# Token-row sums for three entrance norms, roots spread by a product of ones, and a square-root table for the last root

## The chip, the cores and the metric

One core of a Trainium2 chip runs the whole kernel. The metric is the device time of one execution in microseconds, the median of three timed runs. The engines are TensorE (PE; PEld are its weight loads), VectorE (DVE), ScalarE (ACT), GpSimd (POOL) and SyncE (SP), which issues nearly all DMA transfers.

## The reference

The input x has 2048 tokens of 1024 float32 values. One decoder block is computed:

```python
hn = rmsnorm(h, norm1_g)                       # h = x; mean of squares over the 1024 values of a token
proj = einsum('bsd,de->bse', hn, w_in)         # u_pool | q | k | v, 512 each
y_pool = pool_mixer(u_pool, pool_w, pool_scale)
o = stick_breaking_attention(q, k, v)          # 8 heads of 64
mixed = concatenate([rmsnorm(y_pool, pool_out_g), rmsnorm(y_attn, attn_out_g)])
h = h + einsum('bse,ed->bsd', mixed, w_out)
act = square(relu(einsum('bsd,df->bsf', rmsnorm(h, norm2_g), w_up)))
h = h + einsum('bsf,fd->bsd', act, w_down)
return rmsnorm(h, final_g)
# rmsnorm(x, g) = x * rsqrt(mean(x * x) + 1e-6) * g
```

## The kernel before

Tokens are cut into NT = 4 chunks of T = 512, and each chunk into TB = 4 blocks of P = 128. Activations are kept with the channels on the partitions and 512 tokens along the row, so a chunk of x is KD = 8 tiles of 128x512. Every matmul operand is split into a high and a low fp32r part (`split`, L145 to L148: a copy on ScalarE, a subtraction on VectorE), and a product is three matmuls (L179 to L181): one dense step, 24 matmuls of 512 columns, makes 128 output channels of one chunk. Only the needed near part of the attention is computed, unless a check at the end (L1636) asks for the rest; that branch does not run here.

Three stages follow each other: the front (input projection, pooling, near attention and their norms, up to about 500 us), the output projection (`tail`, to about 670 us), and the two feed-forward products (`up`, `down`), whose last steps (`last_steps`) end with the final norm of the last chunk and its output.

A norm over channels works across partitions. In the front, `norm1_rms(j)` squares the eight tiles of a chunk on ScalarE and adds them up on VectorE (`add_square`, L187 to L191). `mean_squares` (L207) multiplies the sum by a column of 1/n with four matmuls of one column, so that each token's mean stands on a partition. `inv_root` (L215 to L226) takes the root by three Newton steps on columns of 128x4, on GpSimd except for the first chunk and the last half. `spread` (L233) brings the four columns back along the rows for all partitions: eight matmuls of 128 columns, with a high and a low part, into one bank, which a ScalarE copy (L258) makes into the factor r. The pieces of h are then x times gain times r (`normed`, L278), split.

The names that the change touches: `norm1_rms` (chunks 1, 2 and 3; chunk 0 has `norm1_first`), `inv_root`, `inv_rms`, `to_all`, `later_rms`, `norm_parts` (the norms of the pooling output for all chunks and of the attention output; for attention chunks 2 and 3 it is called with `make`), `front`, and `last_turn` and `last_steps` in `down`. The accumulators of dense steps are two banks (`psd`), the spreads of the front use `pst` or `psz`, and the pool `ntp` of three 128x512 buffers holds squares and normed tiles alike.

What sets the order: the Tile framework plans every engine's order by priority (program order, raised in `tc.high_priority`) in a simulated timeline, and each engine then runs its list in that order, waiting on semaphores. `tc.issue_after(ins)` places what is written under it behind `ins`, but only on the engine of `ins`. The list `later` holds small steps of the norms; `catch_up` writes one to three of them behind each dense step, behind the last weight split and an earlier evacuation (`done[0]`). `load_x` puts the loads of xT behind the last weight load on SP; nothing else orders loads there but priority, buffers and data. Weights come through two `raw` buffers (SP) and five split granules `hl`, each good for 12 matmuls.

## Time and profile before

| | |
|---|---|
| timed runs, median (lowest to highest) | 1884.99 us (1883.61 to 1886.21) |
| profiled execution, its own time; its span | 1889.78 us; 1888.0 us |
| mean granted clock of TensorE | 0.997 |
| PE busy; PEld | 1863.1 us (99%); 1551.5 us (82%) |
| DVE; ACT; POOL busy | 1471.4 us (78%); 1025.8 us (54%); 226.4 us (12%) |
| DMA moved | 535.91 MB, mean 284 GB/s |
| chain that ended last, by engine | PE 81%, DMA 7%, DVE 7%, ACT 2%, issue 2% |

The page counts a matmul as busy to its modelled end, so neighbouring matmuls overlap, and a PE that is 99% busy can still have short holes; those are listed as waits. What one group of matmuls costs is read from the starts around it. Durations in a group are of single instructions; on ACT and DVE the next one can start before the last has ended.

### The profile page before, as it was taken

What the parts mean: (1) busy time and instruction counts of PE and PEld (TensorE: products, weight loads), DVE (VectorE), ACT (ScalarE), POOL (GpSimd) and SP (SyncE); (2) the same over time, 40 slices, a digit from 0 to 9 for tenths busy, and PEclk for the clock granted to TensorE, in tenths of its full rate; (3) what the DMA queues carried; (4) which work ended last, traced back from release to release, by engine and by line L of the source; (5) the groups of instructions that cost most, each with busy time, mean ns of one, the idle gap of its engine ahead of it and who ended that gap; (6) DMA issues with size and microseconds to landing.
All of it is one profiled execution on the core that took longest, in us unless ns stands there. A gap on an engine that the chain in (4) does not pass through costs nothing.

```text
span 1888.0 us, 26651 instructions
## 1 busy us (share of the span) xinstructions
PE 1863.1 (99%) x8883; PEld 1551.5 (82%) x8883; DVE 1471.4 (78%) x2135; ACT 1025.8 (54%) x1616; POOL 226.4 (12%) x463
## 2 busy tenths in 40 slices
PE   9999999999999999999999999999999999999997
PEld 7888888888888788888888888887888888888886
DVE  6887889678866877878799988886565677989774
ACT  6565666455644454555557555554333665656543
POOL 0232234112311040000000000000010010020120
PEclk9999999999999999999999999999999999999999
DMA  7686796899796858989798988889999898899852
GB/s 227 217 269 187 238 291 204 257 333 302 272 365 227 308 199 292 336 286 321 271 340 304 319 295 286 286 303 335 359 318 316 303 319 307 332 299 346 284 207 92
DMA packets 222164, 535.91 MB, mean 284 GB/s; under 512 B 26048, under 2 KB 32192, under 8 KB 218176
## 3 DMA queue, kind: packets, MB, share of 16 engines
q1 hardware_dynamic: 217264, 525.46, 80.4%
q0 software_dynamic: 4608, 8.39, 2.5%
q8 instruction: 72, 1.18, 0.3%
q14 instruction: 76, 0.62, 0.1%
q10 hardware_dynamic: 144, 0.26, 0.0%
HBM read 349.46 MB, written 184.55 MB: 283 GB/s over the span
## 4 chain that ended last, share of the span: by engine, by line
PE 81%; DMA 7%; DVE 7%; ACT 2%; issue 2%; POOL 1%; SPq 1%; DVEq 0%; ACTq 0%; POOLq 0%
PE pY L1148 17%; PE pb L1321 14%; PE pb L1498 12%; PE pZ L1148 8%; PE pd L179 6%; PE pd L181 6%; PE pd L180 6%; PE pX L1148 4%; PE po L702 1%; DMA ar<-sd 1%; PE pta L690 1%; DMA raw<-in_w_in_dram 1%; DVE hl L148 1%; DMA ar<-sdi 1%; DMA sr<-su 1%
## 5 line engine op out<-in xcount | busy, mean ns | idle before, releaser
L1148 PE MATMUL pY<-sa,hw 128*128 128x512 f32 x1536 | 366.1, 389 | 2.2 <-ACT u L1071 2.1
L1148 PEld LDWEIGHTS pY<-sa,hw 128*128 128x128 f32 x1536 | 287.9, 188 | 63.8 <-ACT u L1071 3.4
L1321 PE MATMUL pb<-ad,wd 128*128 128x512 f32 x1344 | 305.2, 389 | 0.3 <-DVE ad L148 0.3
L179 PE MATMUL pd<-h,hl 128*128 128x512 f32 x752 | 296.9, 395 | 4.4 <-DVE qk L148 2.4
L180 PE MATMUL pd<-h,hl 128*128 128x512 f32 x752 | 296.3, 394 | 0.0
L181 PE MATMUL pd<-h,hl 128*128 128x512 f32 x752 | 295.9, 394 | 0.0
L1321 PEld LDWEIGHTS pb<-ad,wd 128*128 128x128 f32 x1344 | 252.1, 188 | 53.1 <-DVE ad L148 0.7
L1498 PE MATMUL pb<-ad,wd 128*128 128x512 f32 x1104 | 253.9, 390 | 1.6 <-DVE ad L148 0.9
L1498 PEld LDWEIGHTS pb<-ad,wd 128*128 128x128 f32 x1104 | 206.6, 188 | 45.3 <-DVE ad L148 1.7
L148 DVE TENSOR_TENSOR ad<-ar,ad 128x1024 fp32r<-128x1024 f32 x160 | 194.0, 1221 | 38.8 <-ACT ad L147 38.4
L147 ACT ACTIVATE ad<-ar 128x1024 fp32r<-128x1024 f32 x160 | 168.9, 1057 | 93.9 <-PE pb L1498 38.2
L1148 PE MATMUL pZ<-sa,hw 128*128 128x512 f32 x768 | 185.9, 389 | 0.0
L1148 PEld LDWEIGHTS pZ<-sa,hw 128*128 128x128 f32 x768 | 144.0, 188 | 30.2 <-ACT sa L147 0.4
L147 ACT ACTIVATE hl<-raw 128x512 fp32r<-128x512 f32 x168 | 104.2, 629 | 117.6 <-PE pd L181 79.4
L179 PEld LDWEIGHTS pd<-h,hl 128*128 128x128 f32 x752 | 141.7, 188 | 32.0 <-DVE qk L148 2.8
L181 PEld LDWEIGHTS pd<-h,hl 128*128 128x128 f32 x752 | 141.6, 188 | 28.3
L180 PEld LDWEIGHTS pd<-h,hl 128*128 128x128 f32 x752 | 141.8, 189 | 26.1
L148 DVE TENSOR_TENSOR hl<-raw,hl 128x512 fp32r<-128x512 f32 x168 | 114.8, 689 | 50.3 <-ACT hl L147 49.0
L148 DVE TENSOR_TENSOR hw<-rt,hw 128x512 fp32r<-128x512 f32 x128 | 86.8, 686 | 33.1 <-ACT hw L147 33.1
L147 ACT ACTIVATE wd<-wq 128x1024 fp32r<-128x1024 f32 x56 | 59.5, 1063 | 76.1 <-PE pb L1321 65.7
L1065 ACT ACTIVATE a<-a 128x512 f32<-128x512 f32 x96 | 60.0, 629 | 74.1 <-DVE a L1107 35.9
L148 DVE TENSOR_TENSOR wd<-wq,wd 128x1024 fp32r<-128x1024 f32 x56 | 68.4, 1222 | 32.4 <-ACT wd L147 32.4
(224 smaller groups left out, 2712.0 us busy)
## 6 DMA issues: line engine op xcount, KB each, us to landing
ar<-sd SPq DMA_DIRECT2D x96, 512.0 KB, 5.8
ar<-sdi SPq DMA_DIRECT2D x64, 512.0 KB, 5.9
rb<-in_w_up_dram SPq DMA_DIRECT2D x30, 1024.0 KB, 6.8
sd<-a SPq DMA_DIRECT2D x104, 256.0 KB, 5.0
raw<-in_w_in_dram SPq DMA_DIRECT2D x50, 512.0 KB, 4.8
sdi<-hr SPq DMA_DIRECT2D x96, 256.0 KB, 5.2
wr<-in_w_down_dram SPq DMA_DIRECT2D x48, 512.0 KB, 5.5
sd<-s SPq DMA_DIRECT2D x88, 256.0 KB, 4.7
```

The lines of the kernel that those rows point to most:

```text
L147: nc.scalar.activation(hi, src, AF.Copy)
L148: return nc.vector.tensor_tensor(lo, src, hi.bitcast(F32), ALU.subtract)
L179: nc.tensor.matmul(ps, hl[:, 0, c], hi, start=(k == 0), stop=False)
L180: nc.tensor.matmul(ps, hl[:, 0, c], lo, start=False, stop=False)
L181: last_mm[0] = nc.tensor.matmul(ps, hl[:, 1, c], hi, start=False, stop=(k == n - 1))
L690: nc.tensor.transpose(pt[:, x * P:(x + 1) * P], sg[:, x * P:(x + 1) * P], ident)
L702: nc.tensor.matmul(po[0:m, p * 256 + to:p * 256 + to + hi - lo], vw[:, 2 * p + v, 0:m], at[:, x, lo:hi], start=(p == 0 and n == 0), skip_g ...
L1065: nc.scalar.activation(t, src, AF.Relu)
L1148: nc.tensor.matmul(t, w[:, wx, c], a[:, ax, c % 2], start=first and c == 0 and x == 0, stop=last and c == G - 1 and x == 2, skip_group_che ...
L1321: nc.tensor.matmul(b, t[:, wx, 2 * (kk % 2) + c, i * P:(i + 1) * P], a[:, ax, c], start=p in ("P1", "P5", "P2") and kk == 0 and c == 0 and ...
L1498: nc.tensor.matmul(ps[q, n], block(t, wx, c, n), left_[q][:, ax, c], start=(n_ in ("P1", "P3") and kk == 0 and c == 0 and x == 0), stop=(n ...
```

## The change

There are three edits.

First, `norm1_rms` for chunks 1 to 3. x is given a second time, as token rows (`x_rows`, blocks of 128 tokens by 1024 channels). Four loads of 512 KB per chunk go through one buffer (`xr`), and ScalarE squares each in place with a running sum over the row, which gives one column of sums. The root then starts from those four columns with the scale 1/n in its first step, on GpSimd. The eight squares, seven adds and the matmuls of `mean_squares` are left out for these norms. In `front` the note that writes this norm for chunk 1 moves one dense step ahead.

Second, `spread_rows`, for six norms (the pooling output of four chunks, the attention output of chunks 0 and 1). The root's columns are written into a zeroed 128x128 tile; one matmul against the identity turns them into rows, four ScalarE copies masked by a selector make a 128x512 tile that holds only the row of each block, and one matmul with a stationary matrix of ones adds high and low parts and spreads them. All other spreads stay as they were, reading the columns out of the zeroed tile.

Third, `root_by_table`, in `last_steps`: the root of the last norm's two halves takes a square root on ScalarE, a reciprocal and one Newton step on VectorE in place of three Newton steps. A square root of one column is put in front of `last_turn`.

Constants for this (`sel`, `oner`, `eps`, `sums1`, the two zeroed tiles) are made at the start.

```diff
@@ -51,14 +51,18 @@
...
-    wp = hpb = hpa = pa = bigp = x0p = ntp = tmp = att = psd = psx = psz = pst = pso = olp = accp = acc2p = acc3p = None
+    wp = hpb = hpa = pa = bigp = x0p = ntp = tmp = att = psd = psx = psz = pst = pso = olp = accp = acc2p = acc3p = wide = None
 
     def open_pools(scope):
-        nonlocal hpb, wp, tmp, ntp, psd, psx, psz, pst, pso
+        nonlocal hpb, wp, wide, tmp, ntp, psd, psx, psz, pst, pso
         fpool = lambda name, bufs, **kw: scope.enter_context(tc.tile_pool(name=name, bufs=bufs, **kw))
         hpb = fpool("hpb", KD, side="right")
         ntp = fpool("ntp", 3, side="right")
         tmp = fpool("tmp", 2, side="right")
+        wide = [tmp.tile([P, P], F32R, name=f"wide{i}", bufs=1) for i in range(2)]
+        tmp.tile([P, P // 2], F32, name="gap2", bufs=1)
+        for t in wide:
+            nc.gpsimd.memset(t.bitcast(F32), 0.0)
         wp = fpool("wp", 2, side="right")
         psz = fpool("psz", 2, space=PS)
         pso = fpool("pso", 1, space=PS)
@@ -96,7 +100,11 @@
     make_identity(nc, ident)
     identr = const.tile([P, P], F32R, name="identr")
     nc.vector.tensor_copy(identr, ident)
-    const.tile([P, P // 2], F32, name="gap")
+    const.tile([P, P // 2 - 40], F32, name="gap")
+    sel = const.tile([P, TB], F32, name="sel")
+    nc.vector.tensor_tensor(sel, ident[:, 0:TB], ident[:, TB:2 * TB], ALU.add)
+    oner = const.tile([P, TB], F32R, name="oner")
+    nc.vector.tensor_scalar(oner, sel, 0.0, 1.0, op0=ALU.mult, op1=ALU.add)
     later_keys = const.tile([P, 2, 2, P], mybir.dt.int8, name="later_keys")
     nc.gpsimd.memset(later_keys, 0.0)
     for i in range(2):
@@ -120,6 +128,9 @@
     rlast = const.tile([P, 2, T], F32, name="rlast")
     sslast = const.tile([P, T], F32, name="sslast")
     yrlast = const.tile([P, 2, 2, TB], F32R, name="yrlast")
+    sums1 = const.tile([P, NT, TB], F32, name="sums1")
+    eps = const.tile([P, 8], F32, name="eps")
+    nc.vector.memset(eps, EPS)
     carry = const.tile([P, len(WINDOWS), PAD], F32, name="carry")
     nc.vector.memset(carry, 0.0)
     window_sum = const.tile([P, len(WINDOWS)], F32, name="window_sum")
@@ -208,11 +219,11 @@
                                                start=(i == 0), stop=(i == len(parts) - 1))
         return pm[:, 0:TB]
 
-    def inv_root(pm, eng):
+    def inv_root(pm, eng, scale=None):
 
         v, w = vp.tile([P, 3 * TB], F32, tag="v", name="v"), pm.shape[-1]
         m, y, t = v[:, 0:w], v[:, TB:TB + w], v[:, 2 * TB:2 * TB + w]
-        nc.vector.tensor_scalar(m, pm, 1.0, EPS, op0=ALU.mult, op1=ALU.add)
+        (eng if scale else nc.vector).tensor_scalar(m, pm, scale or 1.0, EPS, op0=ALU.mult, op1=ALU.add)
         eng.tensor_scalar(y.bitcast(I32), m.bitcast(I32), -0.5, float(0x5F3759DF), op0=ALU.mult, op1=ALU.add)
         for _ in range(3):
             if eng is nc.vector:
@@ -226,6 +237,18 @@
                 eng.tensor_tensor(y, y, t, ALU.mult)
         return y
 
+    def root_by_table(pm):
+
+        v, w = vp.tile([P, 3 * TB], F32, tag="v", name="v"), pm.shape[-1]
+        m, y, t = v[:, 0:w], v[:, TB:TB + w], v[:, 2 * TB:2 * TB + w]
+        nc.scalar.activation(t, pm, AF.Sqrt, bias=eps[:, 0:1])
+        nc.vector.tensor_scalar(m, pm, 1.0, EPS, op0=ALU.mult, op1=ALU.add)
+        nc.vector.reciprocal(y, t)
+        nc.vector.scalar_tensor_tensor(t, y, -0.5, y, op0=ALU.mult, op1=ALU.mult)
+        nc.vector.tensor_tensor(t, t, m, ALU.mult)
+        nc.vector.scalar_tensor_tensor(y, t, 1.5, y, op0=ALU.add, op1=ALU.mult)
+        return y
+
     def spread(pr, yr):
 
         for b in range(TB):
@@ -234,37 +257,55 @@
                                       start=(b == 0 and x == 0), stop=(b == TB - 1 and x == 1), skip_group_check=True)
         return mm
 
+    def spread_rows(pr, yr, r):
+
+        nc.tensor.matmul(pr[:, 0:P], yr, identr, start=True, stop=True)
+        z = ntp.tile([P, T], F32R, tag="nt", name="roots")
+        for b in range(TB):
+            nc.scalar.activation(z[:, b * P:(b + 1) * P], pr[:, 0:P], AF.Copy, scale=sel[:, b:b + 1])
+        mm = nc.tensor.matmul(pr, oner[:, 0:1].to_broadcast([P, P]), z, start=True, stop=True)
+        nc.scalar.activation(r, pr, AF.Copy)
+        return mm
+
     def inv_rms(ss, n, r=None, eng=None, early=False):
 
         eng = eng or nc.gpsimd
         with tc.high_priority():
-            y = inv_root(mean_squares([ss], n, psz if early else None, "pz" if early else "px"), eng)
-            yr = tmp.tile([P, 2, TB], F32R, tag="yr", name="yr")
+            rows = ss.shape[-1] == TB
+            y = inv_root(ss, eng, 1.0 / n) if rows else inv_root(
+                mean_squares([ss], n, psz if early else None, "pz" if early else "px"), eng)
+            wide.append(wide.pop(0))
+            yr = wide[0][:, 0:2 * TB].rearrange("p (x b) -> p x b", x=2)
             eng.tensor_copy(yr[:, 0], y)
             eng.tensor_tensor(yr[:, 1], y, yr[:, 0].bitcast(F32), ALU.subtract)
             if eng is nc.vector:
                 return to_all(yr, r, psx, "px")
-            gates.append((state["tick"] + 10, marks["pm"]))
-            return yr
-
-    def to_all(yr, r, where, tag):
+            if not rows:
+                gates.append((state["tick"] + 10, marks["pm"]))
+            return wide[0]
+
+    def to_all(yr, r, where, tag, rows=False):
         with tc.high_priority():
             pr = where.tile([P, T], F32, tag=tag, name="pr")
-            marks["pr"] = spread(pr, yr)
-            if tag != "px":
-                gates.append((state["tick"] + 12, marks["pr"]))
             if r is None:
                 r = tmp.tile([P, T], F32, tag="r", name="r", bufs=2)
-            nc.scalar.activation(r, pr, AF.Copy)
+            if not rows:
+                marks["pr"] = spread(pr, yr[:, 0:2 * TB].rearrange("p (x b) -> p x b", x=2) if tag != "px" else yr)
+                if tag != "px":
+                    gates.append((state["tick"] + 12, marks["pr"]))
+                nc.scalar.activation(r, pr, AF.Copy)
+            else:
+                marks["pr"] = spread_rows(pr, yr, r)
+                gates.append((state["tick"] + 12, marks["pr"]))
             return r
 
-    def later_rms(at, key, ss, n, r=lambda: None, early=False):
+    def later_rms(at, key, ss, n, r=lambda: None, early=False, rows=False):
 
         got = {}
         where = (psz, "pz") if early else (pst, "pt")
         later.append(lambda: got.update(yr=inv_rms(ss(), n, early=early)))
         later.append(None)
-        later.append(lambda: at.update({key: to_all(got["yr"], r(), *where)}))
+        later.append(lambda: at.update({key: to_all(got["yr"], r(), *where, rows)}))
 
     def rms(chunks):
         return inv_rms(sum_squares(chunks), len(chunks) * P)
@@ -363,11 +404,19 @@
         st[0]["r"] = inv_rms(ss, D, root_tile(), nc.vector)
 
     def norm1_rms(j):
-        def square(k):
-            if k == 0:
-                st[j]["ss"] = sum_tile()
-            add_square(st[j]["ss"], st[j]["x"][:, k], k == 0)
-        later.extend(lambda k=k: square(k) for k in range(KD))
+        got = st[j]["ss"] = sums1[:, j - 1]
+        t = {}
+
+        def load(b):
+            t[b] = pa.tile([P, D], F32, tag="xr", name="xr", bufs=1)
+            nc.sync.dma_start(t[b], x_rows[j, b])
+
+        def square(b):
+            nc.scalar.activation(t[b], t[b], AF.Square, accum_out=got[:, b:b + 1])
+            if b + 1 < TB:
+                load(b + 1)
+        later.append(lambda: load(0))
+        later.extend(lambda b=b: square(b) for b in range(TB))
         later_rms(st[j], "r", lambda: st[j]["ss"], D, lambda: root_tile() if j == 2 else None, j == 1)
 
     def norm1(j):
@@ -437,7 +486,7 @@
             add_square(st[j]["sm"], part(k), k == 0)
         later.extend(lambda k=k: square(k) for k in range(4))
         where = lambda: olp.tile([P, T], F32, tag="ra", name="ra", bufs=1) if make else None
-        later_rms(st[j], "rm", lambda: st[j]["sm"], D // 2, where)
+        later_rms(st[j], "rm", lambda: st[j]["sm"], D // 2, where, rows=not make)
         if make:
             return lambda: normed(4, part, g, make, lambda: st[j]["rm"])
         normed(4, part, g, make_st, lambda: st[j]["rm"], mx[j][at:at + 4])
@@ -534,8 +583,10 @@
         for i, c in enumerate((EARLY if q else FIRST) + POOL):
             if q == 0 and i == 2:
                 note(lambda: load_x(b, x0p))
+            if q == 0 and i == 3:
+                note(lambda: norm1_rms(b))
             if q == 0 and i == 4:
-                note(lambda: (norm1_rms(b), catch_up(len(later)), norm1(b)))
+                note(lambda: (catch_up(len(later)), norm1(b)))
             if q == 0 and i == 8:
                 note(lambda: (catch_up(len(later)), to_att(), load_x(b + 1, bigp)))
                 attend(a, 0)
@@ -1392,6 +1443,7 @@
 
             lastv["res"] = res = [rlp.tile([P, 2, 2, T], F32, tag="rl", name="res") for _ in range(2)]
             half = [bank(b) for b in range(4)]
+            nc.scalar.activation(vp.tile([P, 3 * TB], F32, tag="v", name="v")[:, 0:1], ones, AF.Sqrt, bias=eps[:, 0:1])
             for n in range(4):
                 t = tmp_.tile([P, T], F32, tag="sq", name="fs")
                 nc.scalar.activation(t, lastv["c"][n], AF.Copy, scale=gf[:, n:n + 1])
@@ -1420,7 +1472,7 @@
                     lo = th * W + i * P
                     nc.tensor.matmul(pm[:, i:i + 1], ss[:, lo:lo + P], inv[D], start=True, stop=False)
                     nc.tensor.matmul(pm[:, i:i + 1], sq[:, i * P:(i + 1) * P], inv[D], start=False, stop=True)
-                y = inv_root(pm[:, 0:2], nc.vector)
+                y = root_by_table(pm[:, 0:2])
                 for i in range(2):
                     b = 2 * th + i
                     o = lastv["res"][th][:, i]
@@ -1669,6 +1721,7 @@
     chunks = lambda g: g.reshape(-1, P).T
     arrays = {
         "xT": a["x"].reshape(NT, T, KD, P).transpose(0, 3, 2, 1),
+        "x_rows": a["x"].reshape(NT, TB, P, D),
         "gains": _np.concatenate([chunks(a[n]) for n in ("norm1_g", "norm2_g", "final_g", "pool_out_g",
                                                          "attn_out_g", "pool_scale")], axis=1),
         "w_in": cols(a["w_in"]),
```

## Rows read from the trace of the kernel before

**Rows 1.** Waits of PE, whole span: who waited for whom, us, times, longest.
```profile
PE pd L179 <- DVE qk L148: 2.4, 2, 1.4
...
PE pd L179 <- DVE acc L844: 1.8, 1, 1.8
...
PE pr L233 <- POOL yr L1366: 0.9, 1, 0.9
```

**Rows 2.** Timeline of PE, four places: start us, length us, engine, line, operation.
```profile
56.50 0.95 PE L207 MATMUL pm<-inv,ss 128*128 128x1 f32 x8
57.31 0.47 PE L180 MATMUL pd<-h,hl 128*128 128x512 f32 x1
...
66.79 1.00 PE L233 MATMUL pr<-identr,yr 128*128 128x128 f32 x8
67.63 0.45 PE L179 MATMUL pd<-h,hl 128*128 128x512 f32 x1
...
86.15 0.39 PE L180 MATMUL pd<-h,hl 128*128 128x512 f32 x1
86.38 0.39 PE L181 MATMUL pd<-h,hl 128*128 128x512 f32 x1
...
546.44 0.22 PE L233 MATMUL pr<-identr,yr 128*128 128x128 f32 x1
546.50 0.44 PE L181 MATMUL pd<-h,hl 128*128 128x512 f32 x1
```

**Rows 3.** Groups by line and shape: busy us, mean ns, idle before.
```profile
L191 DVE TENSOR_TENSOR ss<-ss,sq 128x512 f32<-128x512 f32 x73 | 49.6, 685 | 3.2 <-ACT sq L190 2.4
...
L190 ACT ACTIVATE sq<-xt 128x512 f32<-128x512 f32 x28 | 16.9, 627 | 1.8 <-DVE ss L191 1.2 <-ACT sq L190 0.4
...
L147 ACT ACTIVATE ad<-ar 128x1024 fp32r<-128x1024 f32 x160 | 168.9, 1057 | 93.9 <-PE pb L1498 38.2 <-PE pb L1321 27.4 <-DMA ar<-sd 17.4
...
L425 ACT ACTIVATE yb<-pp,gains 128x512 f32<-128x512 f32 x16 | 11.0, 686 | 6.5 <-PE pp L424 6.5
...
L1452 ACT ACTIVATE fsh<-u,gains 128x256 f32<-128x256 f32 x6 | 3.0, 494 | 0.0
```

**Rows 4.** Timeline of SP's queue in the first 20 us.
```profile
12.19 1.85 SPq L322 DMA_DIRECT2D xt<-in_xT_dram  x4
```

**Rows 5.** Timeline of ACT, five places; idle before in brackets.
```profile
19.14 0.63 ACT L187 ACTIVATE ss<-xt 128x512 f32<-128x512 f32 x1
...
67.83 0.60 ACT L258 ACTIVATE r<-pr 128x512 f32<-128x512 f32 x1
...
88.46 1.28 ACT L648 ACT_TABLE_LOAD   x1
...
1861.28 2.07 ACT L1401 ACTIVATE res<-pb 128x512 f32<-128x512 f32 x4 [4.37 <-PE pb L1399]
...
1879.50 1.27 ACT L1428 ACTIVATE res<-pb,v 128x512 f32<-128x512 f32 x2 [2.11 <-DVE v L221]
```

**Rows 6.** DMA issues from 0 to 130 us: size of each, median us to landing.
```profile
raw<-in_w_in_dram SPq DMA_DIRECT2D x15, 512.0 KB, 4.2
xt<-in_xT_dram SPq DMA_DIRECT2D x8, 512.0 KB, 8.1
```

**Rows 7.** Timeline of DVE, three places.
```profile
51.24 0.69 DVE L191 TENSOR_TENSOR ss<-ss,sq 128x512 f32<-128x512 f32 x1
...
81.91 1.29 DVE L148 TENSOR_TENSOR h<-nt,h 128x512 fp32r<-128x512 f32 x2
...
1877.28 0.16 DVE L215 TENSOR_SCALAR v<-pb 128x2 f32<-128x2 f32 x1 [0.37 <-PE pb L1422]
```

**Rows 8.** Stretches: busy of each engine, then PE's granted clock, DMA share, GB/s.
```profile
25.00:40.00 15.00, 15.00 (x76) 12.73 (x75) 8.29 (x24) 4.95 (x9) 0.00 (x0) 1.00 0.35 107
40.00:66.00 26.00, 26.00 (x124) 21.62 (x123) 22.98 (x43) 12.04 (x21) 8.24 (x19) 1.00 0.92 282
...
661.00:665.00 4.00, 3.95 (x11) 3.11 (x12) 4.00 (x7) 2.87 (x4) 3.99 (x1) 0.58 0.76 267
```

More of the change, by code (lines that the diff above doesn't have):

```diff
@@ L45, in hymba_block @@
 @with_exitstack
-def hymba_block(ctx: ExitStack, tc: tile.TileContext, xT, gains, w_in, pool_w, w_out, w_up, w_down, out):
+def hymba_block(ctx: ExitStack, tc: tile.TileContext, xT, x_rows, gains, w_in, pool_w, w_out, w_up, w_down, out):
     nc = tc.nc
```

## Prediction

> **What bounds the kernel now.** I read the busy shares first, then TensorE's waits, then the stream of its matmuls. PE is busy 99% of the span (the table), and the longest groups of its waits come to 2.4, 1.8 and 0.9 us [rows 1]. In the stream a matmul of 512 columns starts 0.23 us after the one before it (86.15 to 86.38 [rows 2]). So the time is a sum of matmuls plus a few holes. An edit on VectorE, ScalarE, GpSimd or a queue counts only where it makes or fills a hole in PE's stream; an edit that takes matmuls out counts at once, where they stood. The one stretch of another kind is the very end, where PE has finished and a serial chain runs on VectorE and ScalarE.
>
> **Part 1: entrance norms 1 to 3 by token rows.** Removed from PE: for each of three norms the group of L207, eight passes in the trace. In the stream one such group starts at 56.50 and the dense matmul behind it at 57.31: 0.81 us [rows 2]. Three of them, on the path, because the stream is full on both sides: a gain of 2.4.
>
> Removed elsewhere: 3 x 7 = 21 adds of 0.685 us on VectorE, 14.4 us, and 3 x 8 = 24 squares of 0.627 us on ScalarE, 15.0 us [rows 3]. Added: 12 squares of 1024 columns. The trace has no such activation with a running sum; the nearest is the 1024-column copy of 1.057 us [rows 3], so 12.7 us, and with as much as a half of that again for reading the sum out, 19. ScalarE so stands between 2.3 us relieved and 4 us more loaded, spread over some 300 us in which it is busy about 60%. I take zero for both engines, since PE hides them. The scaling step of the root goes from VectorE to GpSimd: zero.
>
> Added on SP and the DMA engines: 12 loads of 512 KB, 6.3 MB. They have one buffer, so a load leaves only after the square of the one before, four times in series for each norm, and everything queued behind it on SP (weights, stores of q, k and v, attention's operands) waits with it. Likewise each square stands in ScalarE's queue ahead of weight splits. Norms 2 and 3 are early enough for that. For norm 1 it matters when the first load leaves. It waits for no computed value, and the code ties it to no other instruction. The loads of xT for the same chunk, which are tied to the last weight load, left at 12.19 [rows 4] and its first square ran at 19.14 [rows 5], long before the step at which the code puts the norm (about 30 us). So I take the first row load to leave near 8 to 14 us as well. One turn is a landing (in the first 130 us xT's loads had a median of 8.1 us, weights 4.2 [rows 6]; I take the middle, 6.2) plus 1.06 us: four turns of 7.2 us end at about 40. Before, the last add ended at 51.24 + 0.69 = 51.9 [rows 7]. From 25 to 40 us the DMA engines have room, with a share of 0.35 [rows 8]. The cost at the start is one row load in front of the third and fourth weight blocks, by bounds from nothing to its own length at 282 GB/s, 1.9 us [rows 8]; I take nothing, because weights are split some granules ahead of their use.
>
> An earlier sum could also give something. r of norm 1 was ready at 67.83 + 0.60 = 68.4 [rows 5], the last piece of its h at 81.91 + 1.29 = 83.2 [rows 7], and the two dense steps that use it or fill in for it ended at about 86.4 [rows 2]. PE stood in them for about 0.3 us only, so I count nothing and keep 0 to 1.
>
> **Part 2: six roots spread by a product of ones.** Before, one spread is eight matmuls of 128 columns, 66.79 to 67.63: 0.84 us [rows 2]. After, it is one matmul of 128 columns (a lone one cost 0.06 us, 546.44 to 546.50) and one of 512 (0.23): 0.29. Six times 0.55 is a gain of 3.3. Between the two stand four masked copies of 128x128 on ScalarE, with a pointer for scale. 512 columns of that kind take 0.686 and 256 take 0.494 [rows 3]; halving again gives an estimate of 0.40 each, 9.6 us for 24, with bounds of 0.12 (a quarter of the 256) and 0.49. They lengthen the way to r by some 1.5 us. The six norms (four of the pooling, two of the attention) write to DRAM and are read again only in the output projection, so nothing that PE needs is late next. The second matmul does wait for the copies. I take it that other matmuls are planned in between, as they are around the near attention, whose steps alternate between PE, ScalarE and VectorE all through this stage and give none of the longest waits. The price if not is a rival below. The two zeroed tiles and the selectors are made in the first 3 us, before PE has data: nothing.
>
> **Part 3: the last root.** Before: from the first VectorE step at 1877.28 [rows 7] to the scaled copy at 1879.50 [rows 5], 2.22 us for eleven steps and a hand-over, 0.2 each at most. After: a root on ScalarE and four VectorE steps, 0.8, with two hand-overs of 0.1. The root on 128x2 has no row: between 0.16 (a VectorE step of that size [rows 7]) and 0.49 (256 columns with a pointer [rows 3]); I take 0.3. Together 1.3, a gain of 0.9, between 0.7 and 1.1, on the path whole, since the last output transfers leave behind it. The same edit at the earlier half frees the output queue sooner, so the last transfers don't meet it.
>
> The square root wants a table. One table load takes 1.28 us [rows 5]; squares and copies ran before it and after it with no further load, so they run under both tables. The change loads the new one ahead of the last transposes, where ScalarE was idle 4.37 us [rows 5]: I count nothing. The Trainium skill, "ScalarE: Activation LUTs", section "What ACT_TABLE_LOAD costs", speaks against it: a change of set costs about 2.66 us, load and drain together. By that figure one change would still lie in the idle time and the sum would stand; paid once more inside the last chain, it would turn the third part into a loss of 1.8 us and the sum into 3.9. No run here shows it.
>
> **Sum.** 2.4 + 3.3 + 0.9 = 6.6 us. The profiled run took 1889.8 us (span 1888.0), 4.8 above the median of the three timed runs. So 1889.8 becomes 1883.2 in a profile, and 1885.0 becomes **1878.4** in timed runs.
>
> **Rivals.** The order of every engine's work is planned anew, so holes move; each rival names a place.
>
> Copies that hold PE. If the product of ones comes next in PE's order, PE stands for the copies: four at a spacing of about 0.3 and as much for the hand-overs, 1.5 us, six times 9. That gives 1878.4 + 9 = 1887, no difference; for part of them, 1881 to 1886. For it: the one spread in the trace that was planned too early made PE stand 0.9 us for GpSimd's root, though dense matmuls were queued behind it [rows 1]. The Trainium skill, "TensorE: Matmul & The Clock Gate", section "Step-by-step: what each phase is for", says that only weight loads are pulled ahead and matmuls keep their order; that wait agrees. Against: it is the only wait of a spread among all nineteen.
>
> Row loads that come late (slower). If norm 1's first row load leaves only at its place in the code, behind the stores of q and k at about 44 us, into a stretch in which the DMA share is 0.92 [rows 8], four turns of 7.2 us end at 73. The root took from 57.3 to 66.8 [rows 2] and r 1.6 more, so r would come at 82 to 84, 14 to 16 us late. The dense steps have 3.2 us between the last piece of h and their end, and there are two accumulators, so little can stand in: a hole of about 11 us. Holes also cost clock: behind the 1.8 us hole at 661 us, the mean clock of four microseconds was 0.58 [rows 8], the lower of the two levels, 1.2 GHz, for 3.4 of them, another 1.7 us. 1878.4 + 11 + 1.7 = 1891. The mechanism decides from r at 71.6; at 78.2 it eats the whole gain, and with the clock's loss the change is measurably slower from r at about 80.5.
>
> More than the sum. VectorE is short of 14.4 us of adds, and the front's holes at VectorE's door (2.4 and 1.8 us [rows 1], with the clock's 1.7) may close: up to 6 more, 1872.
>
> The change not doing what it says: if the row sums still went by matmul, 2.4 would be missing, 1880.8. The code leaves little for that.
>
> **How the numbers follow.** Forecast 0.55 (from 1875 to 1881.5 with the bounds above), more than the sum 0.10, copies that hold PE 0.18, late row loads 0.16, not as it says 0.01. About 0.2%, 3.8 us, is what a measurement can tell from no change: faster means below 1881.2, slower above 1888.8. Faster: nearly all of the first two, 0.62. Slower: most of the late loads and a little of the copies, 0.16. The rest, 0.22, is the same. The range goes from the low rival's 1872 to 1888; it leaves out the late loads' upper part and the edge of the low rival, some 0.18.
>
> **What would show it.** Right: 24 L207 passes and 48 spread passes fewer, with 12 new matmuls; dense steps that come earlier by an amount that grows to about 5.7 us at 600 us; 1.3 us from the last VectorE root's start to the scaled copy; one more table load, in idle time. Wrong: r of norm 1 later than 71 us; PE waits on the product of ones that name the copies; ScalarE or SP standing for row loads with PE waits on weight splits behind them; or holes in the front that grew by as much as the matmuls shrank.

## The result, and the profile after

The changed kernel takes 1889.93 us (median of nine runs, 1887.83 to 1893.38) against 1885.80 for the kernel before beside it (nine runs, 1883.61 to 1888.72): a ratio of 1.0022, with an interval of 1.0012 to 1.0031. It is slower by 0.2%, and 1.9 us above the upper end of the range. The profiled execution took 1888.30 us (span 1886.6). The profiled execution of before, 1889.78 us, was slower than all nine of its timed runs, so the two profiles understate the loss; experiment e3, which plans the order of before up to about 1830 us, stands beside them below.

**What was to become shorter did.** Groups of PE and ScalarE in the changed kernel (busy us, mean ns, idle before them): L218 has 120 passes where L207 had 144; 64 + 24 spread passes on rolling tiles where there were 136; six products of ones (L266), for which no wait is listed. L218 are the product groups, L256 the spreads, L262 the passes that turn columns into rows.

```profile
L218 PE MATMUL pm<-inv,ss 128*128 128x1 f32 x120 | 14.2, 239 | 0.0
L256 PE MATMUL pr<-identr,wide 128*128 128x128 f32 x64 | 8.3, 266 | 0.0
L256 PE MATMUL pr<-identr,yr 128*128 128x128 f32 x24 | 3.3, 268 | 0.9 <-POOL yr L1417 0.9
L266 PE MATMUL pr<-roots,oner 128*128 128x512 f32 x6 | 2.4, 396 | 0.0
L262 PE MATMUL pr<-identr,wide 128*128 128x128 f32 x6 | 1.5, 254 | 0.5 <-POOL wide L280 0.5
...
L415 ACT ACTIVATE xr<-xr 128x1024 f32<-128x1024 f32 x12 | 12.7, 1058 | 8.2 <-DMA xr<-in_x_rows_dram 8.2
L265 ACT ACTIVATE roots<-pr,sel 128x128 fp32r<-128x128 f32 x24 | 6.8, 372 | 6.6 <-PE pr L262 6.6
```

**What PE waits for** (whole span: us, times, longest) is where the time went. In place of 2.4 and 1.8 us at the head of the list [rows 1] stand 6.8 and 3.8:

```profile
PE pd L190 <- DVE qk L159: 6.8, 2, 6.0
PE pr L256 <- POOL yrlast L902: 3.8, 1, 3.8
```

The timeline of PE shows the two places (start us, length us, engine, line, operation; idle before in brackets). Behind the first, a matmul of 512 columns starts 0.43 us after the last, where 0.23 is usual [rows 2].

```profile
242.49 0.46 PE L753 MATMUL po<-at,vw 128*64 128x128 f32 x4
248.91 0.80 PE L190 MATMUL pd<-h,hl 128*128 128x512 f32 x1 [5.96 <-DVE qk L159]
249.50 0.63 PE L191 MATMUL pd<-h,hl 128*128 128x512 f32 x1
249.93 0.63 PE L192 MATMUL pd<-h,hl 128*128 128x512 f32 x1
...
690.73 0.67 PE L256 MATMUL pr<-identr,yrlast 128*128 128x128 f32 x5
691.23 0.68 PE L1199 MATMUL pX<-sa,hw 128*128 128x512 f32 x2
695.67 1.39 PE L256 MATMUL pr<-identr,yrlast 128*128 128x128 f32 x5 [3.76 <-POOL yrlast L902]
696.86 5.29 PE L1199 MATMUL pY<-sa,hw 128*128 128x512 f32 x12
```

**The hole at 692 us.** The planner put five passes of the second spread of tile yrlast behind two matmuls of pX, while GpSimd was still at its root. The rows of GpSimd (the tile's two halves end the list; the row of VectorE is its last before them) show that the root ended at 695.9. In the kernel before, the same spread stands whole, behind 24 matmuls of pZ at 710.9, and waits for nothing: its root ended at 697.8, 13 us ahead (the last two rows).

```profile
690.20 1.06 POOL L234 TENSOR_TENSOR v<-v 128x4 f32<-128x4 f32 x1
...
695.16 0.20 POOL L237 TENSOR_TENSOR v<-v 128x4 f32<-128x4 f32 x1
695.43 0.19 POOL L902 CAST yrlast<-v 128x4 fp32r<-128x4 f32 x1
695.69 0.20 POOL L903 TENSOR_TENSOR yrlast<-v,yrlast 128x4 fp32r<-128x4 f32 x1
...
693.46 1.28 DVE L159 TENSOR_TENSOR hw<-rt,hw 128x512 fp32r<-128x512 f32 x2
```

```profile
697.64 0.20 POOL L852 TENSOR_TENSOR yrlast<-v,yrlast 128x4 fp32r<-128x4 f32 x1
...
710.88 1.00 PE L233 MATMUL pr<-identr,yrlast 128*128 128x128 f32 x8
```

**The hole at 243 us.** Both accumulators of the dense products are full (the code has two), and the evacuation that frees one (qk, a copy on ScalarE and a step on VectorE) stands on ScalarE behind two chunks of the pooled branch's norm (mix) and four passes of attention (at, sh, sg, ot). The mix chunks wait for transfers: mix, qk, vt and pls share one ring of three tiles (st), and a tile is free only when its store has landed. The first rows are of ScalarE in the changed kernel, the last three of the kernel before (ScalarE, then PE). There the first mix chunk stands at the same time, behind the same store, and qk 1.2 us earlier; PE comes to the same product (the 817th large one in both) 2.5 us later, with 28 matmuls more behind it, and waits 1.4.

```profile
242.22 0.63 ACT L158 ACTIVATE mix<-nt 128x512 fp32r<-128x512 f32 x1 [1.92 <-DMA vs<-vt]
...
244.00 0.63 ACT L158 ACTIVATE mix<-nt 128x512 fp32r<-128x512 f32 x1 [0.63 <-DMA mx<-mix]
244.53 0.58 ACT L158 ACTIVATE at<-pta 128x512 fp32r<-128x512 f32 x1
245.01 0.59 ACT L699 ACTIVATE sh<-pz 128x512 f32<-128x512 f32 x1
245.49 0.60 ACT L701 ACTIVATE sg<-pz 128x512 f32<-128x512 f32 x1
246.11 0.59 ACT L710 ACTIVATE ot<-po 64x512 f32<-64x512 f32 x1
246.73 0.60 ACT L158 ACTIVATE qk<-pd 128x512 fp32r<-128x512 f32 x1
```

```profile
242.15 0.63 ACT L147 ACTIVATE mix<-nt 128x512 fp32r<-128x512 f32 x1 [1.98 <-DMA vs<-vt]
...
245.55 0.58 ACT L147 ACTIVATE qk<-pd 128x512 fp32r<-128x512 f32 x1
...
246.90 0.50 PE L179 MATMUL pd<-h,hl 128*128 128x512 f32 x1 [1.41 <-DVE qk L148]
```

**The clock behind both.** Stretches of the changed kernel (busy of each engine, then granted clock, DMA share, GB/s): during and behind each hole.

```profile
243.00:249.00 6.00, 0.09 (x1) 0.09 (x1) 5.37 (x8) 4.68 (x9) 1.27 (x2) 0.91 1.04 354
249.00:255.00 6.00, 6.00 (x19) 4.84 (x20) 0.69 (x1) 1.16 (x2) 0.00 (x0) 0.52 1.01 387
...
691.00:695.60 4.60, 0.91 (x6) 0.47 (x5) 3.74 (x6) 3.04 (x6) 3.96 (x9) 0.94 0.33 119
695.70:702.00 6.30, 6.30 (x18) 5.19 (x19) 0.00 (x0) 0.00 (x0) 0.19 (x1) 0.51 0.00 0
```

PE is full behind each hole, but for some six microseconds at about half clock (0.52 and 0.51, the 1.2 GHz level): about 3 us lost again each time, on top of the holes.

**The end.** Timeline of ScalarE: the table load is in idle time, 44 us ahead of the last root (38 ahead of the first half's), and the last root takes from 1877.32 to 1878.53.

```profile
1833.70 1.28 ACT L1446 ACT_TABLE_LOAD   x1
1835.00 0.30 ACT L1446 ACTIVATE v<-ones,eps 128x1 f32<-128x1 f32 x1
...
1877.32 0.26 ACT L244 ACTIVATE v<-pb,eps 128x2 f32<-128x2 f32 x1 [1.03 <-PE pb L1474]
1878.53 1.26 ACT L1480 ACTIVATE res<-pb,v 128x512 f32<-128x512 f32 x2 [0.94 <-DVE v L249]
```

**Where the time is, kernel by kernel.** The next table is worked out from the starts of all matmuls of a trace. A gap that is over 0.25 us longer than the usual one for its width counts as a hole by what it has too much; a 512-column matmul that is drawn out by 0.06 to 0.25 us counts as slow clock; the rest is called matmul work. The front is the time to the 2201st of the 7536 large products (matmuls of 256 columns or more on tiles pd, pX, pY, pZ, pb), the stretch behind it goes to the 2401st. One profiled execution each.

```
us                      before    e3   change    e1     e2     e4     e9    e12
front, to product 2201   651.8  652.4   650.9  648.1  655.1  650.7  652.1  663.6
  of it holes              8.0    7.3    12.1    7.4   13.0   12.6   12.5   15.4
  of it slow clock         4.1    5.0     5.8    3.9    5.6    5.3    5.1    7.4
  of it matmul work      639.7  640.1   633.0  636.8  636.5  632.8  634.5  640.8
to product 2401           50.9   49.0    56.1   47.2   51.7   47.8   47.2   47.2
```

Against e3, the front's matmul work shrank by 7.1 us and its holes and slow clock grew by 5.6. About 0.8 of the 7.1 is a product group of eight passes that only stands behind product 2201 now. The 50 us around 692 take 7.1 us more than in e3; some 1.3 of these are that group and five spread passes that e3 has further on, the rest is the hole and the slow clock.

### The profile page after: what moved, and what is told of

Same layout as the page of the kernel before. It is cut to its first block, busy times and chain, and to the rows that moved or that the text cites. A ratio compares the mean times of both kernels' runs of the same rounds, so it can differ in the third digit from the quotient of the medians.

```text
span 1886.6 us, 26556 instructions
## 1 busy us (share of the span) xinstructions
PE 1859.1 (99%) x8823; PEld 1548.5 (82%) x8823; DVE 1458.5 (77%) x2102; ACT 1033.5 (55%) x1644; POOL 216.4 (11%) x468
## 4 chain that ended last, share of the span: by engine, by line
PE 85%; DMA 5%; DVE 5%; ACT 2%; issue 1%; POOL 1%; SPq 0%; DVEq 0%; ACTq 0%; POOLq 0%
PE pY L1199 18%; PE pb L1372 16%; PE pb L1550 11%; PE pZ L1199 9%; PE pd L190 7%; PE pd L192 7%; PE pd L191 7%; PE pX L1199 4%; PE po L753 1%; PE pta L741 1%; DMA xt<-in_xT_dram 1%; DVE hl L159 1%; DMA rb<-in_w_up_dram 1%; PE pz L693 1%; PE pz L694 1%
```

## Experiments

Each time is a median of timed runs with before beside it on the same chip; the ratio's interval is in brackets.

**e1, e2, e3: one part alone**, the other two undone, the tiles of the change kept. The three pairs of lines undo part 2 (in e1 and e3), part 3 (in e1 and e2) and part 1 (in e2 and e3, with the squares of before).

```diff
-        later_rms(st[j], "rm", lambda: st[j]["sm"], D // 2, where, rows=not make)
+        later_rms(st[j], "rm", lambda: st[j]["sm"], D // 2, where)
-                y = root_by_table(pm[:, 0:2])
+                y = inv_root(pm[:, 0:2], nc.vector)
-        later.extend(lambda b=b: square(b) for b in range(TB))
+        later.extend(lambda k=k: square(k) for k in range(KD))
```

> Only part 1 of the change (row sums for the entrance norms of chunks 1 to 3; the six spreads and the last root as before; the new tiles stay). Theory A, the re-planned order: the three product groups really go (-2.4 us of TensorE work), but the later start (some 1.2 us more of small holes before 10 us) and a hole of 4 to 6 us near 243 us behind the new order on ScalarE, with half clock after it (3.4 us), eat them: 1886 to 1892 us against 1885.8, and no 3.8 us hole near 692 us. Theory B, the parts' own work costs: 12 passes of 1.06 us on ScalarE and 6.3 MB of transfers cost wherever the queue is full, so the loss is spread over many small holes, and no single hole is over 3 us: 1887 to 1890. Theory C, the prediction's sum holds for this part and the loss belongs to another: 1883.4.

> Only part 2 (six spreads by one product of ones from masked copies; the entrance sums and the last root as before). Theory A: the spreads give 3.3 us, and the second spread of the last chunk's root (tile yrlast), now planned 18 us earlier and split 5 + 3, waits 3.8 us for GpSimd near 692 us and is followed by half clock for 6.8 us (3.4 us): 1885.8 - 3.3 + 7.2 = 1889.7, range 1887 to 1891; that hole in the trace. Theory B: the masked copies (24 passes of 0.37 us on ScalarE) hold TensorE at each spread: 1887 too, but with waits at the product of ones and none over 3 us elsewhere. Theory C: sum holds, 1882.5.

> Only part 3 (last root from the square-root table). All theories: 0.9 us less at the end of the kernel, nothing else moves, since the order of the engines before the last rows hardly differs: 1884.9 against 1885.8. If the new tiles of the change (their places in SBUF) cost anything, this run shows it too: above 1885.8.

Measured: e1 1881.32, 0.9983 (0.9972 to 0.9993); e2 1891.82, 1.0041 (1.0027 to 1.0055); e3 1884.83, 1.0003 (0.9994 to 1.0012), before 1884.86. Part 1 gains 3 us (0.17%; 2.4 were foreseen), and neither its row loads nor the hole of theory A eat that. Part 3 cannot be told from nothing in these times. The traces show its gain: from the start of the last large product to the end of the span they take 11.5 us in e3 and 13.0 in before (10.9 to 12.2 in all twelve profiles with part 3, 12.8 to 13.5 in the five without). The loss belongs to part 2: foreseen as -3.3 us, measured as 7.7 slower. Waits of PE in e2, with the hole near 692 us that theory A foresaw, then in e1, whose hole near 243 us is 2.7 us and not 6:

```profile
PE pr L256 <- POOL yrlast L892: 2.6, 1, 2.6
```

```profile
PE pd L190 <- DVE qk L159: 3.1, 2, 2.7
```

Theory A came near e2's total with other terms than the trace has: the hole is 2.6 us and not 3.8, and the granted clock behind it stayed at 1.00. In this execution it is a good third of the loss; the front's holes, 13.0 us against 7.3 in e3, are another part.

**e4: the last spread held.** All three parts; the two spreads of yrlast may not be planned ahead of the group of matmuls behind which the code writes them. **e10** is the counterpart on another order: the edit of e9 below without this hold.

```diff
-                    nc.tensor.matmul(t, w[:, wx, c], a[:, ax, c % 2], start=first and c == 0 and x == 0,
+                    mm_ = nc.tensor.matmul(t, w[:, wx, c], a[:, ax, c % 2], start=first and c == 0 and x == 0,
...
-                spread(pr, yrlast[:, i])
+                with tc.issue_after(mm_.ins):
+                    spread(pr, yrlast[:, i])
```

> The whole change, with the two spreads of tile yrlast held behind the last matmul of the group at which they are written, so that they cannot be planned earlier. Theory A: the hole of 3.8 us near 692 us goes and with it the half clock after it (3.4 us): 7 us less than the changed kernel's 1889.9, so 1882.7, range 1881 to 1885. Theory B (the loss is spread over the kernel, the hole at 692 us is only where a slip shows): under 2 us is won, 1888 to 1890, and the same time turns up in holes further on.

> As e9_rows3_later, but the last spread not held (as in the change). Theory A: e9 plus the 7 us of the hole near 692 us and its half clock: 1881 to 1884, with the change's 1889.9 less 6 to 8. If the two holes are not independent (the earlier one shifts the later), the difference to e9 is under 4 us.

Measured: e4 1881.65, 0.9986 (0.9977 to 0.9995), and e10 1890.62, 1.0025 (1.0015 to 1.0036) against e9's 0.9986. The hold is worth 0.36% (1.0022 to 0.9986, each against before on its own chip) in one order and 0.39% in the other, 6.8 and 7.4 us, as theory A said of the difference; e10's own time missed its range because e9's did. In e4 the spreads stand whole, with no idle time before them, after a root that ended at 695.7 (PE timeline), and the matmuls of pY that stood behind the split spread run ahead of it:

```profile
701.23 1.00 PE L256 MATMUL pr<-identr,yrlast 128*128 128x128 f32 x8
702.08 5.66 PE L1199 MATMUL pZ<-sa,hw 128*128 128x512 f32 x24
707.58 1.00 PE L256 MATMUL pr<-identr,yrlast 128*128 128x128 f32 x8
```

This hole alone turns the change from a gain into a loss. It came with the second part: of the runs without the hold, the three with part 2 (the change, e2, e10) have the split spread, and those without it (before, e1, e3, e8, e12, e13, e14) don't. No run has part 2 with just one other part and no hold.

**e9, e11, e5: the hole at 243 us**, each on top of e4. e9 begins chunk 3's norm six dense steps later; e11 sums chunk 3 from x's tiles, as before; e5 gives st four tiles (bufs=4 for mix, pls, qk and vt too), by taking the row tiles from that ring. The edits in this order:

```diff
-            note(lambda: (load_x(b, bigp), norm1_rms(b), norm1(b), pace(2)))
+            note(lambda: (load_x(b, bigp), pace(2)))
...
+            if q and i == 6:
+                note(lambda: (norm1_rms(b), norm1(b)))
```

```diff
+        if j == 3:
...
+            later.extend(lambda k=k: square_x(k) for k in range(KD))
+            later_rms(st[j], "r", lambda: st[j]["ss"], D)
+            return
```

```diff
-            t[b] = pa.tile([P, D], F32, tag="xr", name="xr", bufs=1)
+            t[b] = pa.tile([P, D], F32, tag="st", name="xr", align_bytes=256, bufs=4)
```

> The whole change, last spread held as in e4_last_spread_held, and the entrance norm of chunk 3 (its four row loads, row squares and the norm) begun six products later, so that no row load and no row square lies near 243 us; there ScalarE then has the evacuation qk right behind the last of the normed chunks. Theory A (chunk 3's rows, squared and loaded among the stores of the pooled branch, push the evacuation behind four more ScalarE passes and its store tile later): the 6.2 us hole falls to 2 to 3 us and TensorE keeps its full clock behind it, 6 to 8 us under e4's 1881.65: 1874 to 1877. Theory B (the hole comes from TensorE arriving earlier at a place that is fixed by the stores): hole of 4 us or more stays, 1880 to 1883. Theory C (the hole goes, and chunk 3's norm, now later, opens another of its size): as B, with the hole elsewhere before 420 us.

> The whole change with the last spread held, but chunk 3's entrance sums as before (eight squares of x and a product group; row sums for chunks 1 and 2 only). Theory A: no row load near 243 us, so the hole there falls to 2 to 3 us at full clock; one product group (0.8 us) comes back: 1875 to 1878. Theory B: hole of 4 us or more, 1881 to 1884.

> The whole change with the last spread held (as e4_last_spread_held, 1881.65 us), and the tiles of x rows taken from the ring st, which then has four tiles in place of three (the same SBUF). Theory A: the 6.2 us hole near 243 us comes about because the evacuation of dense products (tile qk) needs a tile of st, and the three are held by the stores of the pooled branch's normed chunks; with a fourth the evacuation stands right behind the last of these chunks on ScalarE, the hole falls below 2 us and the half clock after it (3.4 us) goes too: 1872 to 1877. Theory B: the hole comes from the transfers themselves (row loads of 512 KB among the stores, each landing late), and a tile more changes nothing: a hole of over 4 us stays, 1879 to 1883.

Measured: e9 1883.79, 0.9986 (0.9977 to 0.9995); e11 1882.48, 0.9986 (0.9975 to 0.9998); e5 1883.96, 0.9992 (0.9983 to 1.0001). None is faster than e4 by the ratio. The hole itself does shrink: in e11 the evacuation follows the second mix by 1.57 us and not 2.73 (ScalarE's timeline), and PE's longest wait for qk is 2.5 us; in e9 it is 2.7.

```profile
242.54 0.63 ACT L158 ACTIVATE mix<-nt 128x512 fp32r<-128x512 f32 x1 [0.58 <-DVE sg L743]
...
244.11 0.57 ACT L158 ACTIVATE qk<-pd 128x512 fp32r<-128x512 f32 x1
```

But the time comes back elsewhere. In e9 PE now waits for chunk 3's root (waits of PE, e9):

```profile
PE pd L190 <- DVE qk L159: 5.2, 3, 2.7
PE pr L256 <- POOL wide L279: 2.2, 1, 2.2
```

In e11 large product 901 starts 3.1 us earlier than in e4, product 1101 only 1.0 and product 2201 0.2 later: PE arrives early and waits for attention's VectorE steps at 324, as it does in before and e3; e4 doesn't wait there at all (timeline of PE, e11):

```profile
323.80 0.44 PE L749 MATMUL pta<-ident,sg 128*128 128x128 f32 x2 [0.52 <-DVE at L159]
325.50 0.62 PE L761 MATMUL po<-at,vw 128*128 128x256 f32 x4 [0.70 <-DVE ot L719]
```

In e5 the row tiles share the ring, and PE waits at 138 and 149 us instead, 2.5 and 2.0 us (waits of PE, e5):

```profile
PE pd L190 <- DVE qk L159: 3.5, 3, 1.9
PE po L753 <- DMA vw<-vs: 2.3, 1, 2.3
```

So each theory A is right that its edit shrinks the hole at 243 us and wrong on the price: taking the hole away gains nothing that the runs can show.

**e7, e6, e14, e15: the ring, with the row tiles gone.** e7 has parts 2 and 3 with the last spread held; e6 gives the room of the row tile to st, which has four tiles; e14 has the ring of four with part 3 alone; e15 is e6 with row sums for chunk 1 only, from two tiles in a pool that closes early. The ring (mix, pls and vt alike) and then e15's rows:

```diff
-        d = pa.tile([P, 2, T], F32R, tag="st", name="qk", align_bytes=256, bufs=3)
+        d = pa.tile([P, 2, T], F32R, tag="st", name="qk", align_bytes=256, bufs=4)
...
+                t[b] = x0p.tile([P, D], F32, tag="xr", name="xr", bufs=2)
+                nc.sync.dma_start(t[b], x_rows[j, b])
...
+                if b + 2 < TB:
+                    load(b + 2)
```

> Parts 2 and 3 without the row sums, last spread held. The sum of the prediction holds where no order slips: 1884.9 - 3.3 (six spreads) - 0.5 (last root, from e3's 0 and the 0.9 foreseen) = 1881, and 1 us more if the hole near 246 us is 2.4 us as in e2_spreads_alone in place of 1.4: range 1880 to 1883. If part 2 has a cost of its own beside the misplaced spread (copies on ScalarE), 1884 to 1887.

> Parts 2 and 3 without the row sums, last spread held, and st with four tiles (the room of the row tile). Against e7_no_sums_three it changes the ring alone. Theory A: the hole of 2 to 2.5 us near 246 us that these kernels have goes: 1.5 to 2.5 us under e7, some 1879.5. Theory B (transfers): as e7.

> Part 3 alone (e3_last_root_alone, 1.0003 of before) with the ring st of four tiles in place of three; no spread and no sum changed. If the ring limits the front's evacuations whatever the norms do, the hole near 247 us (1.56 us) and those of qk tiles elsewhere fall and it is 1.5 to 3 us faster than before: 1882.5 to 1884. If the ring only mattered for the orders that the change brings: as before, 1885 to 1886.

> As e6_no_sums_four (parts 2 and 3, last spread held, four tiles of st; 0.9973 of before), and the row sums for chunk 1 alone, from two row tiles in a pool that closes before attention opens. One product group (0.8 us) and 8 squares fewer: 0.9969 of before, some 1879. If the row loads among the first weights cost (first 60 us), or the new order opens a hole, 1880 to 1884.

Measured: e7 1884.50, 0.9995 (0.9986 to 1.0004); e6 1879.70, 0.9973 (0.9962 to 0.9983); e14 1885.14, 0.9996 (0.9984 to 1.0008); e15 1880.49, 0.9965 (0.9951 to 0.9979). e7 missed its 1880 to 1883 and falls to the other branch, a cost of part 2 beside the split spread. In e7's trace part 2's order has a wait of 1.5 us near 140 us that the ring of four takes away, and PE waits for qk 2.4 us against 1.8 in e6. With the order of before (e14) the fourth tile takes the hole near 247 us away as well, and the time does not move: what the ring is worth depends on the order that meets it. e15 is the best version run, 0.35% under before and 0.57% under the change; its lead over e6 is within the intervals.

**e8: parts 1 and 3.**

> Parts 1 and 3, the spreads as before. If parts add where the order does not slip: 1881.3 (e1_sums_alone) less 0 to 0.9 = 1880.4 to 1881.3. If the 1881.3 of e1 was luck of an order that part 3 shifts again, 1884 or more.

Measured: 1881.02, 0.9978 (0.9969 to 0.9987), as foreseen: the parts add. Up to the last rows e8 plans the very order of e1, so their two profiles show what one order does in two executions: e1 reaches product 2201 at 648.1 us and e8 at 652.9. Both have the hole behind mix, 2.7 and 3.0 us; behind it the clock stayed full in e1 and fell in e8 (stretches, e1 then e8):

```profile
247.00:250.00 3.00, 3.00 (x14) 2.50 (x15) 1.76 (x2) 1.44 (x4) 1.29 (x2) 1.00 1.03 420
```

```profile
247.70:251.00 3.30, 3.29 (x9) 2.64 (x10) 1.77 (x2) 1.51 (x4) 1.29 (x2) 0.61 1.02 409
```

A single trace therefore can't settle a front's holes and slow clock to better than some 5 us; the table of the fronts is to be read with that.

**e12, e13: the order alone.** No part of the change. The gates that hold dense products behind a norm's product group or spread act four steps earlier (e12) or, those behind a spread alone, two later (e13: + 14).

```diff
-                gates.append((state["tick"] + 10, marks["pm"]))
+                gates.append((state["tick"] + 6, marks["pm"]))
-                    gates.append((state["tick"] + 12, marks["pr"]))
+                    gates.append((state["tick"] + 8, marks["pr"]))
```

> No part of the change, and no work added or taken away: only the gates that keep dense products behind a norm's product group and spread stand four steps earlier, so that the front's order is planned anew (about 500 of 8800 matmuls, 130 of 1620 ScalarE passes stand elsewhere). Theory A (a new order by itself opens and closes holes of TensorE in the front worth some us): over 2 us from before in either sense, with the sum of holes before 650 us changed by as much, 1881 to 1890. Theory B (the holes of the changed kernel come from its own copies, row loads and squares): within 1 us of before's 1885.7.

> As e12_order_alone with the gates two steps later, by which only some 90 matmuls and 25 ScalarE passes between 60 and 180 us stand elsewhere. Theory A: under 1.5 us from before, since little moves. Theory B: within 1 us.

Measured: e12 1896.23, 1.0052 (1.0036 to 1.0068); e13 1885.78, 0.9998 (0.9987 to 1.0009). With no work added, an order is 0.5% worse (waits of PE, e12):

```profile
PE pm L218 <- DVE ss L202: 3.2, 2, 1.9
PE po L743 <- DVE ot L701: 2.7, 2, 2.0
...
PE ptv L507 <- DVE vt L159: 1.6, 1, 1.6
```

3.2 us of these are the tighter gates' own doing, since they bring PE to a product group before its sum is there; the waits of po and ptv are work that merely stands elsewhere. A small move (e13) costs nothing.

## Why the prediction was wrong

**The sizes were right.** The starts of the matmuls, holes apart, give the product groups and spreads of the front 24.0 us in e3 and 17.5 in the change. With the 0.8 that only moved taken off, 5.7 us are gone, and 5.7 were worked out; part 1 alone takes out 2.5 (2.4 foreseen) and part 2 alone 2.9 (3.3). The last root takes 1.21 us where 1.3 were foreseen, from 2.22. The table load took 1.28 us in idle time and its first user followed 0.02 later. The Trainium skill, "ScalarE: Activation LUTs", section "What ACT_TABLE_LOAD costs", gives about 2.66 us for load and drain together; the trace shows the load at 1.28 us and no time of a drain behind it.

**The rivals named with a place did not happen.** The product of ones has no wait (the pass ahead of it has one, 0.5 us for GpSimd); its copies take 0.37 us, with 0.40 taken, and other matmuls run between the two (106.5 and 112.2 us for the first pair). The first row load left at 8.92 us (8 to 14 foreseen), the fourth square ended at 38.5 (about 40), and r of norm 1 was there at 49.5, 19 us earlier than before [rows 5] and 22 before the point at which it would have begun to cost.

**The step that failed** is the sum: it took 2.4 + 3.3 + 0.9 us from a time whose holes were held as they were, by the prediction's rule that "an edit that takes matmuls out counts at once, where they stood". The term that did not hold is the 3.3 us of part 2: alone, part 2 is 7.7 us slower (e2). The step that part 1 rests on, "I take zero for both engines, since PE hides them", is not contradicted where part 1 stands alone: e1 gives 3 us. What the runs showed in place of the sum: the new order puts five passes of a spread ahead of GpSimd's root, a hole of 3.8 us with slow clock behind it, together 6.8 and 7.4 us by e4 and e10; some 4 us more are missing without it (e4's 2.6 us of gain against 6.6).

The prediction said that "the order of every engine's work is planned anew, so holes move", and then gave a loss by that a price only at the two places it had thought of. It held two clues. One was the wait of 0.9 us of a spread for GpSimd's root [rows 1], "planned too early": just this struck the spread of yrlast. 12 matmuls of pY stood behind its five passes for 3.76 us; in e4, without the passes ahead of them, they ran at once. The Trainium skill, "TensorE: Matmul & The Clock Gate", section "Step-by-step: what each phase is for", says that matmuls keep their program order and only weight loads are pulled ahead; the trace agrees. The other clue was in the list of what would show it wrong, "holes in the front that grew by as much as the matmuls shrank". That is what the table shows, holes and slow clock up by 5.6 us, in one trace of each kernel. It had no chance of its own among the rivals.

**What stays open.** Without the hole at 692 us the change is worth 0.14% (e4), some 2.6 us of the 6.6 (0.9 to 4.3 by the interval). Part 3's gain shows in the traces, so the rest is put down to the front; that is argued from one trace of each kernel. The largest hole there, at 243 us, is explained, but the three versions that shrink it are no faster than e4. Their traces show other holes in its place (at 315 us in e9, 324 in e11, 138 and 149 in e5), which need not be all that came back. Whether some other engine's chain sets a floor for the front, or each of these orders met holes of its own, the runs don't tell apart; the variation of one order between executions is as large as the difference looked for.

## What to carry to other kernels

Where a planner orders the work, a change of 0.3% must be priced with its new order: look at every product that a small slow chain feeds (here a root on GpSimd), and tie it behind the work that must cover it, since moving it up by 19 us cost about as much as all three edits gave. When matmuls are taken out of a full stream, ask at the next evacuation what frees its buffer: TensorE comes earlier, the store it waits for does not. And compare edits by timed ratios, not by the holes of one trace.

## What the runs showed of the hardware

- Behind holes of 3.8 and 6.0 us TensorE ran at the 1.2 GHz level for about six microseconds. Behind 2.7 to 3.0 us it did so in e8 (0.61) and not in e1 (1.00), on the same order; behind 2.6 us at 698 us in e2 it stayed at 1.00, and behind 1.8 us in the kernel before it fell (0.58 [rows 8]). So the length of a hole alone doesn't tell.
- GpSimd's steps of the root on 128x4 took 0.51 to 1.06 us while VectorE was busy, and 0.19 to 0.20 from 694.89 on, when VectorE had stopped (its last step ended at 694.74). So the root took 9.3 us (686.61 to 695.9). The Trainium skill, "GPSIMD Engine Reference", section "Key points", says that GpSimd contends with VectorE instructions that have two inputs in SBUF; the trace agrees.
- Two loads of an activation table, at 75 and 1834 us, took 1.28 us each, with the activation before ending 0.02 us or less ahead and the next one starting 0.02 or less behind.
- Reading out the running sum of a square is an instruction of its own on ScalarE, 0.18 to 0.19 us behind each 1.06 us pass.
